# A hybrid encoder block on one core: attention on the normed latent, row sums through DRAM, squares on GpSimd

## The chip, the cores and the metric

The kernel runs on one core of a Trainium2 chip. A core has five engines with instruction queues of their own: TensorE (PE in the profile, its weight loads as PEld), VectorE (DVE), ScalarE (ACT), GpSimd (POOL) and SyncE (SP), which in this kernel issues all DMAs. The metric is the time of one execution in device microseconds, as a median over runs. All tensors are f32.

## The reference

One encoder layer, on 2048 tokens of 1024 features:

```python
h = x
xn = rms_norm(h, ln_mix_g)
proj = xn @ w_in            # q, k, v, o: 512 columns each; 16 gates; c_q 256; c_kv 128; k_rope 64
y_a = mlstm_group(...)      # 4 heads of 128, both directions, chunks of 128 tokens
# multi-head latent attention, 4 heads
q = (rms_norm(c_q, q_norm_g) @ w_uq).reshape(b, s, 4, 128 + 64)
kv = (rms_norm(c_kv, kv_norm_g) @ w_ukv).reshape(b, s, 4, 128 + 128)
k_nope, v = kv[..., :128], kv[..., 128:]
sc = q_nope . k_nope + rope(q_rope) . rope(k_rope)     # k_rope is one for all heads
y_b = softmax(sc * (128 + 64) ** -0.5) @ v
h = h + concat(y_a, y_b) @ w_out
h = h + conv_gated_mlp(rms_norm(h, ln_ffn_g), ...)     # 1024 -> 2 x 2816 -> 1024
h = h + sigmoid(rms_norm(h, ple_norm_g) @ w_ple_gate) * rms_norm(p @ w_ple_proj, ple_post_g)
out = rms_norm(h, final_g)
```

Two products of the attention group are linear on both sides. The score q_nope . k_nope of a head is c_q W_uq (W_uk)^T c_kv^T, and what a head adds to h is (softmax @ c_kv) W_uv W_out, where c_kv is the normed latent of 128 columns that all heads share.

## The kernel before

Most products are made with operands split into a high part (ScalarE's cast to fp32r) and a low part (VectorE's subtraction): `split` (L111 to L118) makes the parts, `mm3` (L128) three matmuls from them. The tiles live at named places (`at("w13", ...)`), most with one buffer, so a place that is taken again waits for its last reader. A list scheduler orders each engine's instructions from the program; only in the q and k projection is TensorE's order that of the program. All DMAs stand in SP's one queue, and one that waits holds those behind it.

The stages, in order of time:

- `in_proj`, first part. For each of 16 token tiles of 128, `turn_in` splits the tile of x and `ssq_x` (L224 to L234) makes its mean square: ScalarE squares into `x_sq` (128 features x 8 x 128 tokens, place w13), VectorE sums over the 8 blocks (L229) into `x_ss` (place t7), TensorE sums over the partitions (L231) and GpSimd raises to -1/2 (L234, `rcol`). `rest` (L242 to L269) projects the 464 columns of gates, c_q, c_kv and k_rope, norms c_q and c_kv into `nn` (GpSimd L257, and L136, L138 in `rsq`; VectorE L259, L260) and applies the rope (VectorE L262 to L268). `turn_rest` transposes `nn` and stores it to `rest_d`.
- Then v and o, each 16 token tiles.
- Then q and k: 8 column blocks (j) of 4 token blocks (c), each 24 matmuls, with the convolution over tokens behind them (`conv`). Between the matmuls a side generator is pumped, 1.14 steps at a time: `kv_up`, then `gates`, then `q_up`. `kv_up` loads the latent, projects it with w_ukv to keys (features x tokens, `ko`, stored to `k_d`) and values (tokens x features, `vo2`, stored to `vv_d`) for all heads, 96 matmuls into `gb`. `q_up` does the queries (`q_d`). At j = 7 the keys of head 0 are loaded (`load_kv`) and split (`split_kv`), and a tail behind the loop splits its values.
- `attend` (L823 on): 64 tiles (head h, 128 queries qt). The work of a tile is written out in a string, L912: scores of the next tile (s0 to s3, L849 to L853, with the row maximum L854), exponentials of this and the next (E, e, L872), transposes of the exponentials (t0 to t3, L889, with a split behind each), and V, half of the product with the values for a pair of tiles (`ppv`). At each "." the mLSTM group is pumped. After the fourth exponential the sum over keys is inverted (`ri`, L877, L878) and spread over a row of 128 (`rb`, L881); at R of an odd tile `turn_sums` (L923 to L929) transposes the two `rb` of the pair and copies them to SBUF (`rbs`), and L905 multiplies the finished `ppv` by it and stores it to `y_d`. The keys and values of the next head are loaded and split eight times a head during the head before. The `mk` masks of the mLSTM are made on GpSimd (L765), its `kk` by VectorE (L705) for the products of L712.
- `out_proj`, with the w_out rows loaded and split by `load_wo`, the first four of them during the last head; then the gated MLP (`up`, `down`) and `ple`.

Of the kernel before, what the change touches and what calls it, by code (L numbers as in the profile page):

```python
# [18 lines left out]
P = 128  # L19
# [40 lines left out]
class Block:  # L60
# [4 lines left out]
    def __init__(self, ctx, tc, d):  # L65
# [15 lines left out]
        self.kv = {}  # L81
# [5 lines left out]
        self.k_d = dt([NH, P, S], F32, name="k_d")  # L87
        self.vv_d = dt([NH, P, S], F32, name="vv_d")
# [90 lines left out]
    def in_proj(self):  # L179
# [44 lines left out]
        def ssq_x(st, x_t):  # L224

            sq = self.at("w13", [P, KT, P], name="x_sq")
            nc.scalar.activation(sq, x_t, AF.Square)
            ss = self.at("t7", [P, P], name="x_ss")
            nc.vector.tensor_reduce(ss, sq.rearrange("p k t -> p t k"), axis=AX.X, op=ALU.add)  # L229
            ps = self.pml.tile([P, 4], F32, name="ssp", tag="ml")  # L230
            nc.tensor.matmul(ps, ss, ones, start=True, stop=True)  # L231
# [10 lines left out]
        def rest(st):  # L242
# [17 lines left out]
            nc.vector.scalar_tensor_tensor(nn[:, 256:384], rs[:, 256:384], r[:, 1:2], gn[:, 256:384], op0=ALU.mult, op1=ALU.mult)  # L260
            x1, x2 = rs[:, 384:416], rs[:, 416:448]
# [75 lines left out]
        side, due = chain(self.kv_up(), self.gates(), self.q_up()), 0.0  # L337
# [16 lines left out]
        def pump(due):  # L354
            due += 1.14
            while due >= 1:
                next(side, None)
                due -= 1
            return due
# [12 lines left out]
        with self.tc.manual_schedule(engines={mybir.EngineType.PE}):  # L372
            nxt = load_qk(0)
            for j in range(8):
                ws = nxt
                if j < 7:
                    nxt = load_qk(j + 1)
                else:
                    kr = self.load_kr()
                    kv = [self.load_kv(0, i, w) for i, w in enumerate(("w8", "w13", "w9", "w12"))]  # L380
# [4 lines left out]
                for c in order:  # L385
# [18 lines left out]
                    if j == 7 and c == 1:  # L404
                        for _ in self.split_kv(0, kv, range(2)):
                            pass
# [5 lines left out]
        def tail():  # L412
            for c in (1, 0):
                conv(7, u, c)
                yield
            yield from pause(4)
            yield from self.split_kv(0, kv, range(2, 4))
# [42 lines left out]
    def kv_up(self):  # L460
        nc, d = self.nc, self.d
        wh, wl = self.at("w3", [P, 1024], F32R, "wkh"), self.at("w4", [P, 1024], F32R, "wkl")
        for i in range(2):
            raw = self.at(("t4", "t5")[i], [P, 512], name="wkr")
            fs = slice(i * 512, (i + 1) * 512)
            nc.sync.dma_start(raw, d["w_ukv"][0, :, fs])
            self.split(raw, wh[:, fs], wl[:, fs])
        vw = [w.rearrange("p (h c) -> p h c", h=NH)[:, :, P:2 * P] for w in (wh, wl)]
        orot = _rot("t", (6, 7, 4, 5))

        def load(c):
            raw = self.at(("w8", "w13")[c % 2], [P, 512], name="craw")
            nc.sync.dma_start(raw, self.rest_d[:, 2, c * 512:(c + 1) * 512])
            cc = self.at(("w5", "w7")[c % 2], [P, 2, 512], F32R, "ckv")
            self.split(raw, cc[:, 0], cc[:, 1])
            return cc

        nxt = load(0)
        yield
        for c in range(4):  # L480
            sl = slice(c * 512, (c + 1) * 512)
            ch, cl = nxt[:, 0], nxt[:, 1]
            if c < 3:
                nxt = load(c + 1)
            for h in range(NH):
                ps = self.gbank()
                ws = slice(h * 256, h * 256 + P)
                self.mm3(ps, wh[:, ws], wl[:, ws], ch, cl, True, True)
                o = self.at(next(orot), [P, 512], name="ko")
                nc.scalar.copy(o, ps)  # L490
                nc.sync.dma_start(self.k_d[h, :, sl], o)
                if h % 2:
                    yield
            for t in range(4):
                ps = self.gbank()
                ts = slice(t * P, (t + 1) * P)
                self.mm3(ps.rearrange("p (h c) -> p h c", h=NH), ch[:, ts], cl[:, ts], vw[0], vw[1], True, True)
                o = self.at(next(orot), [P, 512], name="vo2")
                nc.scalar.copy(o, ps)
                tk = slice((c * 4 + t) * P, (c * 4 + t + 1) * P)  # L500
                nc.sync.dma_start(self.vv_d[:, :, tk].rearrange("h p e -> p h e"), o.rearrange("p (h e) -> p h e", h=NH))
                if t % 2:
                    yield
# [319 lines left out]
    def attend(self, side):  # L823
        nc = self.nc
        mm = nc.tensor.matmul
        prot, ptrot = _rot("w", (0, 1, 2)), _rot("x", range(8, 14))
        kv, qv, rbp = self.kv, {}, {}
# [14 lines left out]
        def score_bank(s, kb):  # L842
# [5 lines left out]
            kh, kl = kv[h][0], kv[h][1]  # L848
# [20 lines left out]
        def expo(s, kb):  # L869
# [5 lines left out]
            if kb == 3:  # L875
# [3 lines left out]
                if s.qt % 2 == 0:  # L879
                    rbp[s.h, s.qt // 2] = self.at(f"s{(s.qt // 2) % 2}", [P, 2, P], name="rb")  # L880
                nc.vector.tensor_copy(rbp[s.h, s.qt // 2][:, s.qt % 2, :], ri.broadcast_to([P, P]))  # L881
# [10 lines left out]
        def pv(w, half):  # L892
# [3 lines left out]
            vh, vl = kv[h][2], kv[h][3]  # L896
# [26 lines left out]
        def turn_sums(h, pr):  # L923
            pb = self.tbank([P, 2, P])
            for i in range(2):
                nc.tensor.transpose(pb[:, i, :], rbp[h, pr][:, i, :], self.ident)
            rb = self.at("s2", [P, 2, P], name="rbs")
            nc.scalar.copy(rb, pb)
# [11 lines left out]
        loads = iter(())  # L940
        pts, pend = [], None
        for i, (h, qt) in enumerate(seq):
            if qt == 1 and h + 1 < NH:
                loads = self.split_kv(h + 1, None, range(4))
            next(loads, None)
# [12 lines left out]
            for op in order:  # L958
# [6 lines left out]
                elif op == "R" and qt % 2:  # L965
                    rb = turn_sums(h, qt // 2)
# [586 lines left out]
```

## Time and profile before

| | us |
|---|---|
| median of 3 runs | 3047.44 (3045.35 to 3048.96) |
| the profiled execution | 3049.62 |
| its span, first to last instruction | 3047.8 |
| TensorE busy | 2987.7 (98%) |
| VectorE busy | 1928.1 (63%) |
| ScalarE busy | 1381.3 (45%) |
| GpSimd busy | 138.6 (5%) |

By stage of that execution, in us:

| stretch | what runs | length | TensorE | VectorE | ScalarE | GpSimd |
|---|---|---|---|---|---|---|
| 0 to 97 | `rest` projection | 97 | 84.3 | 80.7 | 63.1 | 31.9 |
| 97 to 270 | v and o | 173 | 169.2 | 40.3 | 30.9 | 3.8 |
| 270 to 530 | q and k, with the side work | 260 | 257.8 | 135.2 | 122.1 | 0.0 |
| 530 to 1280 | attention and mLSTM | 750 | 727.4 | 576.1 | 455.7 | 45.7 |
| 1280 to 1460 | w_out | 180 | 180.0 | 79.9 | 53.7 | 13.4 |
| 1460 to 3047.8 | MLP, `ple` | 1587.8 | 1569.1 | 1015.9 | 656.0 | 43.8 |

In the profile's rows a group reads: line, engine, operation, result <- operands, shapes and count, and then times. A row of a wait reads: engine, what it was about to do, "<-" the work that released it, the sum in us, how often, and the longest. An engine's q (SPq) is its instruction queue, where DMAs are issued. A matmul's duration is that of a pipelined instruction; the distance of two starts is what it costs a full TensorE. An f32 product that is not split stands in the trace as two matmul records. The granted clock of TensorE was 0.997 of full speed on the mean.

### The profile page before, as it was taken

To read this page: it belongs to the slowest core of one execution; us is meant where nothing else is said; L and a number is where in the kernel's file an instruction comes from. 1 tells how busy PE (TensorE), PEld (TensorE's weight loads), DVE (VectorE), ACT (ScalarE), POOL (GpSimd) and SP (SyncE) were. 2 spreads that over 40 slices of the span, in tenths; PEclk is the share of its full clock that TensorE was granted. 3 is DMA by queue.
4 is the path that set the end of the run, shared out by engine and by line. 5 is a ranking of instruction groups with operands and counts; after the bars stand their busy time and mean duration, and the time that the engine had idled before them with its cause. 6 is when DMAs were issued, how large, how long until landed. Compare 5 with 4: busy or idle time off the path is not lost. (4 is left out here: it accounts for less than half of the span.)

```text
span 3047.8 us, 40996 instructions
## 1 busy us (share of the span) xinstructions
PE 2987.7 (98%) x15208; PEld 2520.1 (83%) x15208; DVE 1928.1 (63%) x3527; ACT 1381.3 (45%) x2642; POOL 138.6 (5%) x262
## 2 busy tenths in 40 slices
PE   8999999899999999999999999999999999999999
PEld 7788888788898898888778887788887888888887
DVE  8321555778777787734798888877777343334555
ACT  7212544556666565522544445544444332223444
POOL 3100000000000000000000000000000000000111
PEclk9999999999999999999999999999999999999999
DMA  6522445444333243458763335433336565444221
GB/s 175 114 69 98 149 132 168 143 128 150 101 108 114 95 133 92 137 195 280 255 224 137 135 136 190 145 125 125 124 125 227 166 221 200 145 155 151 78 78 62
DMA packets 332264, 441.03 MB, mean 145 GB/s; under 512 B 25296, under 2 KB 224928, under 8 KB 332064
## 3 DMA queue, kind: packets, MB, share of 16 engines
q1 hardware_dynamic: 332064, 438.42, 44.7%
q8 instruction: 119, 1.95, 0.3%
q14 instruction: 81, 0.66, 0.1%
HBM read 295.84 MB, written 142.50 MB: 144 GB/s over the span
## 5 line engine op out<-in xcount | busy, mean ns | idle before, releaser
L128 PE MATMUL facc<-fw,hid 128*128 128x512 f32 x2112 | 480.7, 390 | 3.0 <-ACT fw L115 1.4
L128 PEld LDWEIGHTS facc<-fw,hid 128*128 128x128 f32 x2112 | 396.2, 188 | 86.6 <-ACT fw L115 1.9
L128 PE MATMUL fxy<-oph,fw 128*128 128x512 f32 x1408 | 450.4, 393 | 7.1 <-DVE ug L1313 4.6
L128 PEld LDWEIGHTS fxy<-oph,fw 128*128 128x128 f32 x1408 | 264.4, 188 | 76.0 <-DVE ug L1313 10.6
L118 DVE TENSOR_TENSOR fw<-fwr,fw 128x1024 fp32r<-128x1024 f32 x176 | 215.2, 1223 | 165.4 <-ACT fw L115 165.4
L115 ACT CAST fw<-fwr 128x1024 fp32r<-128x1024 f32 x176 | 184.7, 1050 | 255.9 <-PE facc L128 131.5
L128 PE MATMUL fxy<-opl,fw 128*128 128x512 f32 x704 | 275.1, 391 | 0.0
L128 PE MATMUL bk<-wsp,xh 128*128 128x512 f32 (+1 forms) x768 | 235.3, 387 | 1.0 <-DVE wsp L124 1.0
L128 PE MATMUL fzs<-oph,fw 128*128 128x512 f32 x704 | 234.5, 390 | 0.0
L115 ACT CAST pt<-tb 128x512 fp32r<-128x512 f32 x256 | 146.1, 588 | 186.4 <-PE tb L889 185.6
L128 PE MATMUL ppv<-pt,kv 128*128 128x256 f32 x1536 | 203.7, 287 | 0.0
L854 DVE TENSOR_REDUCE mx<-bk 128x1 f32<-128x512 f32 x256 | 174.9, 684 | 34.1 <-PE bk L853 33.3
L118 DVE TENSOR_TENSOR pt<-tb,pt 128x512 fp32r<-128x512 f32 x256 | 173.6, 685 | 35.5 <-ACT pt L115 33.9
L128 PEld LDWEIGHTS ppv<-pt,kv 128*128 128x128 f32 x1536 | 188.9, 191 | 0.0
L128 PE MATMUL pgp<-pw,x3s 128*128 128x512 f32 (+1 forms) x792 | 178.7, 385 | 0.0
L872 ACT ACTIVATE pe<-bk,nm 128x512 f32<-128x512 f32 x256 | 173.9, 697 | 10.2 <-DVE nm L866 9.4
L128 PE MATMUL bk<-wo,yhl 128*128 128x512 f32 x744 | 174.3, 392 | 0.0
L128 PE MATMUL bk<-xh,wqk 128*128 128x512 f32 x512 | 169.1, 394 | 0.0
L128 PEld LDWEIGHTS pgp<-pw,x3s 128*128 128x128 f32 x792 | 144.5, 188 | 28.2
L128 PEld LDWEIGHTS bk<-wsp,xh 128*128 128x128 f32 x768 | 144.6, 189 | 27.6 <-DVE wsp L124 2.7
L128 PEld LDWEIGHTS bk<-wo,yhl 128*128 128x128 f32 x744 | 138.4, 188 | 28.1
L128 PE MATMUL bk<-wsp,xl 128*128 128x512 f32 (+1 forms) x384 | 149.7, 390 | 7.9 <-ACT wsp L123 7.3
(321 smaller groups left out, 5465.1 us busy)
## 6 DMA issues: line engine op xcount, KB each, us to landing
fwr<-in_w_down SPq DMA_DIRECT2D x88, 512.0 KB, 3.9
fwr<-in_w_up SPq DMA_DIRECT2D x66, 512.0 KB, 3.9
s_d<-fwr SPq DMA_DIRECT2D x44, 512.0 KB, 3.2
fws<-s_d SPq DMA_DIRECT2D x44, 512.0 KB, 3.6
hraw<-hid_d SPq DMA_DIRECT2D x33, 512.0 KB, 4.8
rw<-row_d SPq DMA_DIRECT2D x32, 512.0 KB, 5.2
hid_d<-fgv SPq DMA_DIRECT2D x22, 512.0 KB, 3.6
hid_d<-fgv SPq DMA_DIRECT2D x22, 511.5 KB, 5.1
```

Of the source, the lines that this page charges most:

```text
L115: nc.scalar.copy(hi, src)
L118: (sub or nc.vector).tensor_tensor(lo, src, _f(hi), op=ALU.subtract)
L128: mm = lambda *a, **k: self.nc.tensor.matmul(*a, **k, skip_group_check=more)
L854: nc.vector.tensor_reduce(s.mx[:, kb:kb + 1], ps, axis=AX.X, op=ALU.max)
L872: nc.scalar.activation(s.pe[:, kb % 2], s.banks[kb], AF.Exp, bias=s.nm, scale=ASCALE, accum_out=s.rs[:, kb:kb + 1])
```

## The change

Three things are changed.

First, `absorb` replaces `kv_up`. It multiplies w_uq's 128 unrotated columns of each head by the head's key weights (8 unsplit f32 products into `gb`, two copies back into `wqr`, which `q_up` then splits as before), and each head's value weights by its 128 rows of w_out (a split of 128x1024, a split of 128x128, two `mm3` of 128x512, copies `woo`, stored to `wo_d`). Attention then takes the normed latent as keys (from `rest_d`) and as values (from `vv_d`, now written tile by tile in `rest` out of `nn`) for all heads: it is split once, in four quarters, and the loads and splits per head are gone. The host hands over w_uq and w_ukv with heads turned. The high and low exponentials `pt` take the places x8, x9, x4 to x7 in place of x8 to x13, and `load_wo` takes x0 to x7 in order and its last four blocks from `wo_d`. The pump's step is 1.17 in place of 1.14.

Second, `turn_sums` is gone: each tile's `ri` (128 x 1) is stored to `ri_d`, and at R of an odd tile a DMA loads the pair's 256 sums back, broadcast over the partitions, into `rbs` (places s0 to s2).

Third, in `ssq_x` three GpSimd additions of 512, 256 and 128 elements a partition stand in place of VectorE's reduction.

In the diff, the removed body of `kv_up` and context are cut; the body stands in the functions above.

```diff
@@ -78,14 +78,14 @@
         dt = self.dram.tile
-        self.kv = {}
         self.qk_d = dt([NT, P, 8, P], F32, name="qk_d")
...
         self.q_d = dt([NH, 8, P, 2, 256], F32, name="q_d")
-        self.k_d = dt([NH, P, S], F32, name="k_d")
-        self.vv_d = dt([NH, P, S], F32, name="vv_d")
+        self.vv_d = dt([P, NT, P], F32, name="vv_d")
+        self.wo_d = dt([NH, P, D], F32, name="wo_d")
+        self.ri_d = dt([NH, NT, P], F32, name="ri_d")
         self.cb_d = dt([NT, P, NH, 129], F32, name="cb_d")
@@ -225,8 +225,11 @@
             nc.scalar.activation(sq, x_t, AF.Square)
+            add = lambda o, a, b: nc.gpsimd.tensor_tensor(o, a, b, op=ALU.add)
+            add(sq[:, 0:4], sq[:, 0:4], sq[:, 4:8])
+            add(sq[:, 0:2], sq[:, 0:2], sq[:, 2:4])
             ss = self.at("t7", [P, P], name="x_ss")
-            nc.vector.tensor_reduce(ss, sq.rearrange("p k t -> p t k"), axis=AX.X, op=ALU.add)
+            add(ss, sq[:, 0], sq[:, 1])
             ps = self.pml.tile([P, 4], F32, name="ssp", tag="ml")
@@ -258,6 +261,7 @@
             nc.vector.scalar_tensor_tensor(nn[:, 256:384], rs[:, 256:384], r[:, 1:2], gn[:, 256:384], op0=ALU.mult, op1=ALU.mult)
+            nc.sync.dma_start(self.vv_d[:, st], nn[:, 256:384])
             x1, x2 = rs[:, 384:416], rs[:, 416:448]
@@ -334,7 +338,7 @@
         H = S // 2
-        side, due = chain(self.kv_up(), self.gates(), self.q_up()), 0.0
+        side, due = chain(self.absorb(), self.gates(), self.q_up()), 0.0
         urot, wrot = _rot("u", (0, 1, 2)), _rot("w", (6, 9, 10, 11))
@@ -352,7 +356,7 @@
         def pump(due):
-            due += 1.14
+            due += 1.17
             while due >= 1:
@@ -377,7 +381,7 @@
                     kr = self.load_kr()
-                    kv = [self.load_kv(0, i, w) for i, w in enumerate(("w8", "w13", "w9", "w12"))]
+                    kv = [self.load_kv(i, w) for i, w in enumerate(("w8", "w13", "w9", "w12"))]
                 u = [self.at(next(urot), [P, H + 2], name="u") for _ in range(2)]
@@ -401,8 +405,8 @@
                         self.split_kr(kr)
-                    if j == 7 and c == 1:
-                        for _ in self.split_kv(0, kv, range(2)):
+                    if j == 7 and c == 2:
+                        for _ in self.split_kv(kv, range(2)):
                             pass
@@ -414,7 +418,7 @@
             yield from pause(4)
-            yield from self.split_kv(0, kv, range(2, 4))
+            yield from self.split_kv(kv, range(2, 4))
@@ -438,79 +442,80 @@
-    def load_kv(self, h, i, place):
+    def load_kv(self, i, place):
...
         raw = self.at(place, [P, 1024], name="kvr")
-        self.nc.sync.dma_start(raw, (self.k_d, self.vv_d)[i // 2][h, :, (i % 2) * 1024:(i % 2) * 1024 + 1024])
+        hs = slice((i % 2) * 1024, (i % 2) * 1024 + 1024)
+        self.nc.sync.dma_start(raw, self.vv_d.rearrange("p k c -> p (k c)")[:, hs] if i // 2 else self.rest_d[:, 2, hs])
         return raw
...
-    def split_kv(self, h, raws, quarters):
-        t = self.kv.setdefault(h, [None] * 4)
+    def split_kv(self, raws, quarters):
         for i in quarters:
-            a = i // 2 * 2
+            a = i // 2
             if i % 2 == 0:
-                t[a:a + 2] = [self.at(f"x{4 - (h % 2) * 4 + a + b}", [P, S], F32R, f"kv{a + b}") for b in range(2)]
-            raw = raws[i] if raws else self.load_kv(h, i, "w13")
+                t = [self.at(f"x{12 - 2 * a + b}", [P, S], F32R, f"kv{a}{b}") for b in range(2)]
+                if a:
+                    self.vh, self.vl = t
+                else:
+                    self.kh, self.kl = t
+            hi, lo = (self.vh, self.vl) if a else (self.kh, self.kl)
             for e in range(2):
                 sl = slice((i % 2) * 1024 + e * 512, (i % 2) * 1024 + e * 512 + 512)
-                self.split(raw[:, e * 512:e * 512 + 512], t[a][:, sl], t[a + 1][:, sl])
+                self.split(raws[i][:, e * 512:e * 512 + 512], hi[:, sl], lo[:, sl])
                 yield
...
-    def kv_up(self):
+    def absorb(self):
         nc, d = self.nc, self.d
...
+        mm = nc.tensor.matmul
+        uq = self.at("w3", [P, NH, 256], name="uqt")
+        nc.sync.dma_start(uq, d["w_uq_turned"])
+        uk, uv = [self.at(("t4", "t5")[i], [P, NH, P], name="ukvt") for i in range(2)]
+        for i, t in enumerate((uk, uv)):
+            nc.sync.dma_start(t, d["w_ukv_turned"][:, i])
+        self.wqr = []
+        for kt in range(2):
+            r = self.at(("w13", "w4")[kt], [P, 768], name="wqr")
+            nc.sync.dma_start(r, d["w_uq"][0, kt * P:(kt + 1) * P, :])
+            self.wqr.append(r)
+
+        def load(h):
+            r = self.at("w8", [P, D], name="wor")
+            nc.sync.dma_start(r, d["w_out"][0, 512 + h * P:512 + (h + 1) * P, :])
+            return r
+
+        raw = load(0)
+        yield from pause(3)
+        for kt in range(2):
+            ps = self.gbank([P, NH, P])
             for h in range(NH):
+                mm(ps[:, h], uq[:, h, kt * P:(kt + 1) * P], uk[:, h], start=True, stop=True)
+            nc.scalar.copy(self.wqr[kt].rearrange("p (h c) -> p h c", h=NH)[:, :, 0:P], ps)
+            yield
+        for h in range(NH):
+            wh, wl = [self.at(t, [P, D], F32R, "woa") for t in ("w5", "w7")]
+            self.split(raw, wh, wl)
+            if h + 1 < NH:
+                raw = load(h + 1)
+            us = self.at(f"s{h % 2}", [P, 2, P], F32R, "uvs")
+            self.split(uv[:, h], us[:, 0], us[:, 1])
+            yield from pause(2)
+            for hf in range(2):
+                fs = slice(hf * 512, hf * 512 + 512)
                 ps = self.gbank()
-                ws = slice(h * 256, h * 256 + P)
-                self.mm3(ps, wh[:, ws], wl[:, ws], ch, cl, True, True)
-                o = self.at(next(orot), [P, 512], name="ko")
+                self.mm3(ps, us[:, 0], us[:, 1], wh[:, fs], wl[:, fs], True, True)
+                o = self.at(f"t{6 + hf}", [P, 512], name="woo")
                 nc.scalar.copy(o, ps)
-                nc.sync.dma_start(self.k_d[h, :, sl], o)
-                if h % 2:
-                    yield
-            for t in range(4):
-                ps = self.gbank()
-                ts = slice(t * P, (t + 1) * P)
-                self.mm3(ps.rearrange("p (h c) -> p h c", h=NH), ch[:, ts], cl[:, ts], vw[0], vw[1], True, True)
-                o = self.at(next(orot), [P, 512], name="vo2")
-                nc.scalar.copy(o, ps)
-                tk = slice((c * 4 + t) * P, (c * 4 + t + 1) * P)
-                nc.sync.dma_start(self.vv_d[:, :, tk].rearrange("h p e -> p h e"), o.rearrange("p (h e) -> p h e", h=NH))
-                if t % 2:
-                    yield
+                nc.sync.dma_start(self.wo_d[h, :, fs], o)
+            yield
...
         for kt in range(2):
-            r = self.at(("w8", "w13")[kt], [P, 768], name="wqr")
-            nc.sync.dma_start(r, d["w_uq"][0, kt * P:(kt + 1) * P, :])
-            w = [self.at(("w3", "w4", "w5", "w7")[2 * kt + i], [P, 768], F32R, "wq") for i in range(2)]
-            self.split(r, w[0], w[1])
+            w = [self.at(("w3", "w5", "w7", "w2")[2 * kt + i], [P, 768], F32R, "wq") for i in range(2)]
+            self.split(self.wqr[kt], w[0], w[1])
             wq.append(w)
@@ -823,8 +828,8 @@
         mm = nc.tensor.matmul
-        prot, ptrot = _rot("w", (0, 1, 2)), _rot("x", range(8, 14))
-        kv, qv, rbp = self.kv, {}, {}
+        prot, ptrot = _rot("w", (0, 1, 2)), _rot("x", (8, 9, 4, 5, 6, 7))
+        kh, kl, qv = self.kh, self.kl, {}
         self.wo = []
@@ -845,7 +850,6 @@
             ps = self.bank()
-            kh, kl = kv[h][0], kv[h][1]
             mm(ps, q[:, 1, o:o + P], kh[:, ks], start=True, stop=False)
@@ -876,9 +880,7 @@
                 nc.vector.reciprocal(ri, ri)
-                if s.qt % 2 == 0:
-                    rbp[s.h, s.qt // 2] = self.at(f"s{(s.qt // 2) % 2}", [P, 2, P], name="rb")
-                nc.vector.tensor_copy(rbp[s.h, s.qt // 2][:, s.qt % 2, :], ri.broadcast_to([P, P]))
+                nc.sync.dma_start(self.ri_d[s.h, s.qt].unsqueeze(1), ri)
@@ -893,7 +895,7 @@
                 w.ps = self.ppv.tile([P, 256], F32, name="ppv", tag="pv")
-            vh, vl = kv[h][2], kv[h][3]
+            vh, vl = self.vh, self.vl
             for kb in (2 * half, 2 * half + 1):
@@ -920,12 +922,10 @@
-        def turn_sums(h, pr):
-            pb = self.tbank([P, 2, P])
-            for i in range(2):
-                nc.tensor.transpose(pb[:, i, :], rbp[h, pr][:, i, :], self.ident)
-            rb = self.at("s2", [P, 2, P], name="rbs")
-            nc.scalar.copy(rb, pb)
+        def sums(h, pr):
+
+            rb = self.at(f"s{pr % 3}", [P, 2, P], name="rbs")
+            self.row_bcast(rb.rearrange("p a t -> p (a t)"), self.ri_d[h, 2 * pr:2 * pr + 2].rearrange("a t -> (a t)"), 2 * P)
             return rb
@@ -937,12 +937,8 @@
             expo(cur, int(o[1]))
-        loads = iter(())
         pts, pend = [], None
         for i, (h, qt) in enumerate(seq):
-            if qt == 1 and h + 1 < NH:
-                loads = self.split_kv(h + 1, None, range(4))
-            next(loads, None)
             if h == NH - 1 and qt in (4, 6, 8, 10):
@@ -963,7 +959,7 @@
                 elif op == "R" and qt % 2:
-                    rb = turn_sums(h, qt // 2)
+                    rb = sums(h, qt // 2)
                 elif op == "X" and nxt:
@@ -1010,8 +1006,8 @@
         raw = self.at("w13" if k < 4 else ("w13", "w12")[k % 2], [P, D], name="wor")
-        nc.sync.dma_start(raw, self.d["w_out"][0, k * P:(k + 1) * P, :])
-        w = self.at(f"x{(k + 4) % 8}", [P, 2, D], F32R, f"wo{k}")
+        nc.sync.dma_start(raw, self.d["w_out"][0, k * P:(k + 1) * P, :] if k < 4 else self.wo_d[k - 4])
+        w = self.at(f"x{k}", [P, 2, D], F32R, f"wo{k}")
         self.split(raw, w[:, 0], w[:, 1])
@@ -1540,6 +1536,10 @@
     turned = lambda a: _np.ascontiguousarray(a.T.reshape(-1, P, S).transpose(1, 0, 2))
+    heads = lambda a, n, o=0: a[0].reshape(-1, NH, n)[:, :, o:o + P].transpose(2, 1, 0)
+    src["w_uq_turned"] = _np.ascontiguousarray(heads(src["w_uq"], 192))
+    ukv = src.pop("w_ukv")
+    src["w_ukv_turned"] = _np.ascontiguousarray(_np.stack([heads(ukv, 256), heads(ukv, 256, P)], axis=1))
     src["g_turned"] = _np.ascontiguousarray(src.pop("ln_mix_g")[0].reshape(KT, P).T)
```

More of the change, by code (lines that the diff above doesn't have):

```diff
@@ L454, in split_kv @@
             for e in range(2):
                 sl = slice((i % 2) * 1024 + e * 512, (i % 2) * 1024 + e * 512 + 512)
-                self.split(raw[:, e * 512:e * 512 + 512], t[a][:, sl], t[a + 1][:, sl])
+                self.split(raws[i][:, e * 512:e * 512 + 512], hi[:, sl], lo[:, sl])
                 yield
-    def kv_up(self):
+    def absorb(self):
         nc, d = self.nc, self.d
-        wh, wl = self.at("w3", [P, 1024], F32R, "wkh"), self.at("w4", [P, 1024], F32R, "wkl")
-        for i in range(2):
[L464 to L478, printed above, removed]
-        yield
[L480 to L484, printed above, removed]
-            for h in range(NH):
@@ L488, in kv_up @@
-                self.mm3(ps, wh[:, ws], wl[:, ws], ch, cl, True, True)
-                o = self.at(next(orot), [P, 512], name="ko")
+                self.mm3(ps, us[:, 0], us[:, 1], wh[:, fs], wl[:, fs], True, True)
+                o = self.at(f"t{6 + hf}", [P, 512], name="woo")
                 nc.scalar.copy(o, ps)
-                nc.sync.dma_start(self.k_d[h, :, sl], o)
-                if h % 2:
-                    yield
-            for t in range(4):
-                ps = self.gbank()
-                ts = slice(t * P, (t + 1) * P)
-                self.mm3(ps.rearrange("p (h c) -> p h c", h=NH), ch[:, ts], cl[:, ts], vw[0], vw[1], True, True)
-                o = self.at(next(orot), [P, 512], name="vo2")
-                nc.scalar.copy(o, ps)
-                tk = slice((c * 4 + t) * P, (c * 4 + t + 1) * P)
-                nc.sync.dma_start(self.vv_d[:, :, tk].rearrange("h p e -> p h e"), o.rearrange("p (h e) -> p h e", h=NH))
-                if t % 2:
-                    yield
+                nc.sync.dma_start(self.wo_d[h, :, fs], o)
@@ L921, in pump @@
                 due[0] -= 1
-        def turn_sums(h, pr):
-            pb = self.tbank([P, 2, P])
-            for i in range(2):
-                nc.tensor.transpose(pb[:, i, :], rbp[h, pr][:, i, :], self.ident)
-            rb = self.at("s2", [P, 2, P], name="rbs")
-            nc.scalar.copy(rb, pb)
+        def sums(h, pr):
+            rb = self.at(f"s{pr % 3}", [P, 2, P], name="rbs")
+            self.row_bcast(rb.rearrange("p a t -> p (a t)"), self.ri_d[h, 2 * pr:2 * pr + 2].rearrange("a t -> (a t)"), 2 * P)
             return rb
```

## The prediction, made before the changed kernel ran

> **What bounds the kernel now.** I read the page's first part, then the table by stage, then what TensorE waited for, and only then the groups that the diff touches.
>
> ```profile
> span 3047.8 us, 40996 instructions
> PE 2987.7 (98%) x15208; PEld 2520.1 (83%) x15208; DVE 1928.1 (63%) x3527; ACT 1381.3 (45%) x2642; POOL 138.6 (5%) x262
> ...
> 10.00:97.00 87.00, 81.64 (x413) 70.28 (x411) 76.74 (x214) 57.60 (x127) 31.25 (x55) 1.00 0.60 158
> ...
> 270.00:530.00 260.00, 257.84 (x1303) 217.42 (x1302) 135.20 (x364) 122.06 (x229) 0.00 (x0) 1.00 0.49 149
> 530.00:570.00 40.00, 30.02 (x150) 24.74 (x150) 29.00 (x66) 24.24 (x52) 0.00 (x0) 0.87 0.48 153
> 570.00:1280.00 710.00, 697.33 (x4759) 627.88 (x4759) 547.10 (x1444) 431.45 (x1173) 45.72 (x64) 1.00 0.37 116
> ```
>
> In the stage rows the busy times stand in the order PE, PEld, DVE, ACT, POOL, then the granted clock. TensorE idles 60 us of 3047.8. So a matmul taken away is worth its pitch wherever it sat in a full queue (270 to 530, 570 to 1280), and work moved between the other engines is worth nothing there. Two places are not full: the stage of the `rest` projection (10 to 97), where VectorE is nearly as busy as TensorE, and the passage into attention (530 to 570). The waits say the same:
>
> ```profile
> PE mb L712 <- DVE kk L705: 6.4, 1, 6.4
> PE ssp L231 <- DVE x_ss L229: 4.7, 10, 1.3
> ```
>
> **Part 1: key and value up-projection folded into the weights.** Gone are the 96 matmuls into `gb` that read `ckv`:
>
> ```profile
> L128 PE MATMUL gb<-ckv,wkh x32: 389/390/390, 291.5 to 326.4; 128*128 128x512 f32 x32
> L128 PE MATMUL gb<-wkh,ckv x32: 388/390/390, 296.7 to 330.5; 128*128 128x512 f32 x32
> ...
> L128 PE MATMUL gb<-ckv,wkl x16: 389/390/390, 291.2 to 325.9; 128*128 128x512 f32 x16
> ...
> L128 PE MATMUL gb<-wkl,ckv x16: 389/390/390, 296.9 to 330.2; 128*128 128x512 f32 x16
> ```
>
> The 0.39 us is a pipelined duration; the price is the start-to-start pitch. In time order around the first of them:
>
> ```profile
> 291.01 0.39 PE L128 MATMUL bk<-xh,wqk 128*128 128x512 f32 x1
> 291.24 0.39 PE L128 MATMUL gb<-ckv,wkl 128*128 128x512 f32 x1
> 291.46 0.61 PE L128 MATMUL gb<-ckv,wkh 128*128 128x512 f32 x2
> ```
>
> 291.01, 291.24, 291.46: 0.225 to 0.23 each, so 96 x 0.227 = 21.8 us. Added are 2 x 3 matmuls of the same 128x512 form per head for `woa`, 24 x 0.227 = 5.4 us, and 8 unsplit f32 products of 128x128 for the query weights. The nearest form is the unsplit f32 product of L774, of which the trace shows two records each:
>
> ```profile
> 703.30 1.06 PE L774 MATMUL mb<-qk 128*128 128x128 f32 x8
> 704.12 0.48 PE L849 MATMUL bk<-kv,q_t 128*128 128x512 f32 x1
> ```
>
> Eight records take 0.82 us, 0.103 each; 16 make 1.6 us, 3.3 if there are four records to a product. Sum of part 1 on TensorE: -21.8 + 5.4 + 1.6 = **-14.8 us**. It lies wholly in the stage 270 to 530, which is 99% full, so I count all of it.
>
> Everything else in part 1 sits off the path: the 16 `ko` and 16 `vo` copies and 24 of the 32 splits of k and v go from ScalarE and VectorE, which have 138 and 125 us to spare in 270 to 530 and 279 and 163 in attention; in come four splits of w_out rows, four small ones and ten copies. From SP's queue 32 stores and 12 reloads of k and v go; eight stores of the new w_out rows come, and 16 stores of `nn` (64 KB) join the `rest` stage, where the DMA share is 0.60. I cost these at nothing; their cover is those idle shares. The pump's step of 1.17 moves side work a few slots earlier in a full queue: nothing.
>
> **Part 2: row sums by way of DRAM.** Gone are `turn_sums`' 64 transposes, 32 copies on ScalarE (L928, below) and 64 broadcast copies on VectorE (L881).
>
> ```profile
> L926 PE MATMUL tb<-ident,rb x64: 269/273/329, 562.6 to 1276.3; 128*128 128x128 f32 x64
> its engine sat idle before it (us, times) until:
>   DVE rb L881: 3.6, 4
>   DVE pt L118: 0.9, 2
> ...
> 628.78 0.38 PE L926 MATMUL tb<-ident,rb 128*128 128x128 f32 x2
> ...
> 629.00 0.28 PE L712 MATMUL mb<-v,kk 128*128 128x129 f32 x1
> ```
>
> A pair takes 629.00 - 628.78 = 0.22 us; 32 pairs make **-7.0 us**. The 4.5 us of idle before them is a wait on VectorE. What is late next is the transposes of `pe` right behind, which need the same VectorE queue, so I count **-3** of it (ends -4.5 and 0).
>
> In its place: a store of 128 sums per tile and a broadcast load per pair, 96 DMAs on SP. The nearest rows:
>
> ```profile
> y_d<-rbs SPq DMA_DIRECT2D x64, 64.0 KB, 1.7
> ...
> gcol<-in_g_turned SPq DMA_DIRECT2D x1, 4.0 KB, 1.6
> ...
> r_d<-rcol SPq DMA_DIRECT2D x1, 8.0 KB, 11.4
> ...
> L905 DVE TENSOR_TENSOR rbs<-rbs,ppv x32: 404/421/423, 579.3 to 1283.1; 128x256 f32<-128x256 f32 x32
> ...
> L928 ACT COPY rbs<-tb x32: 353/372/392, 563.8 to 1276.6; 128x256 f32<-128x256 f32 x32
> ```
>
> `rcol` is 2048 single elements in 11.4 us; 128 of them lie nearer `gcol`'s 1.6. Store and load in a row are then about 1.6 + 1.7 = 3.3 us, at worst 11.4 + 1.7 = 13.1. The first consumer, L905, runs at 579.3, 15.5 us after the copy at 563.8 that the load replaces. So it is hidden unless SP is held up. SP does stand still for long:
>
> ```profile
> SPq L832 <- PE bk L853: 97.4, 24, 13.6
> SPq L743 <- PE mb L789: 67.7, 12, 15.1
> ```
>
> Now the load waits on SP for its own store to land, 1.6 us or more, 32 times, and the loads of `q_t` and of the mLSTM side that stand behind it come that much later; most of them wait longer than that for TensorE anyway. I take **+1** (ends 0 and +10).
>
> **Part 3: squares summed on GpSimd.** Every tile loses one VectorE reduction, and GpSimd gets adds of 512, 256 and 128 elements:
>
> ```profile
> L229 DVE TENSOR_REDUCE x_ss<-x_sq x16: 1935/1990/2019, 11.6 to 86.3; 128x128 f32<-128x1024 f32 x16
> ...
> L765 POOL TENSOR_SCALAR_AFFINE_SELECT mk<-rw x32: 630/636/1314, 689.1 to 1231.3; 128x512 f32<-128x512 f32 x32
> ...
> masks.py:199 POOL TENSOR_SCALAR_AFFINE_SELECT ident<-ident 128x128 f32<-128x128 f32 x1 | 0.3, 292 | 0.1
> ...
> 59.24 1.51 POOL L257 TENSOR_SCALAR ssq<-ssq 128x1 f32<-128x1 f32 x1 [1.60 <-ACT nn L256]
> ...
> 65.94 0.22 POOL L257 TENSOR_SCALAR ssq<-ssq 128x1 f32<-128x1 f32 x1 [0.97 <-ACT nn L256]
> ```
>
> No large two-input add on GpSimd is in the trace. From the one-input pair, 0.636 at 512 and 0.292 at 128, the slope is 0.9 ns an element with 0.18 us fixed: 3 x 0.18 + 896 x 0.9 ns = 1.3 us as the lower end. With two operands read one after the other the slope doubles: 2.15 us, which I take. The stage row gives GpSimd's other work as 31.25 / 16 = 1.95 us a tile, so it has then 4.1 of the 5.4 us that a tile lasts (87 us by 16).
>
> But the two engines get in each other's way: the single-element L257 lasted 1.51 us at 59.24, against 0.22 at 65.94, while VectorE ran its subtractions and rope products of two SBUF operands back to back. Without L229 VectorE works 76.74 / 16 - 1.99 = 2.8 us a tile. If GpSimd had to stand aside for all of that, its tile would be 4.1 + 2.8 = 6.9 us; if for half, 5.5. So the stage stays near its period or goes a little over. VectorE, 88% busy there, loses 2 us a tile, and the 4.7 us that TensorE waits for L229 may go. Bounds: -4.7 below, 16 x (6.9 - 5.4) = +24 above; I take **+3**, the middle of GpSimd's waiting (0.1 to 0.2 us a tile over the period).
>
> The Trainium skill bears on this in "SBUF — State Buffer", section "SBUF: two separate sides": VectorE with two SBUF inputs and GpSimd reading SBUF take a shared port pair by exclusive lock, for a whole instruction. The 1.51 us row agrees. Its "GPSIMD Engine Reference", section 3.1, puts a two-input add at about 2.6 cycles an element; an estimate by that is 896 x 2.6 / 1.2 GHz plus the fixed part, some 2.5 us a tile, and the sum would be up to 6 us higher.
>
> **The passage into attention.** In time order:
>
> ```profile
> 536.49 0.69 DVE L118 TENSOR_TENSOR kv<-kvr,kv 128x512 fp32r<-128x512 f32 x1 [1.79 <-ACT kv L115]
> ...
> 542.33 0.68 DVE L705 SCALAR_TENSOR_TENSOR kk<-kk,cols 128x512 f32<-128x512 f32 x1
> ...
> 546.45 0.63 PE L850 MATMUL bk<-kr,q_t 128*128 128x512 f32 x1
> 546.87 0.63 PE L851 MATMUL bk<-kv,q_t 128*128 128x512 f32 x1
> ...
> 551.23 0.39 PE L850 MATMUL bk<-kr,q_t 128*128 128x512 f32 x1
> ```
>
> VectorE sits with splits of k and v and reaches `kk` at 542.33; TensorE idles 6.4 us and then runs at half pace (starts 0.43 apart instead of 0.23) to about 551, some 4 us more. After the change the splits of head 1 are gone here, but splits of w_out can come in, and the splits of the latent's value half stay. I take **-3** (ends -10 and 0).
>
> **Sum**, against the profiled execution's 3049.6 us (span 3047.8 and 1.8 around it): -14.8 - 7.0 - 3 + 1 + 3 - 3 = -23.8, giving 3025.8. That execution is 2.2 us above the median shown, so the median goes from 3047.4 to **3024 us**. No change means within 0.2%, 6 us.
>
> **Rivals.**
> - *GpSimd becomes the bound of the `rest` stage.* For: the 1.51 us row, and one buffer each for `x_sq` and `x_ss`, so the next square waits for the adds. Against: VectorE has two fifths of its work less there (1.99 of 4.8 us a tile), and part of that reads a single operand. With a tile of 6.4 us it is +16 instead of +3: 3037. It takes back everything from 7.1 us a tile on (26.8 us without this term, by 16, is 1.7 over 5.4), just past the worst of part 3. Chance 0.17.
> - *Row sums come late* (slower). SP held 13 to 15 us, as in the L743 row, ahead of the store or load, plus the 3.3 us use up the 15.5 us; then L905 stands at the head of VectorE's queue, with the maxima and `pt` splits behind it, and TensorE waits for those. It decides from 24.8 / 32 = 0.78 us a pair; at 1 us it gives 3055. Against: SP's waits end when TensorE moves on, and only a pair whose stall falls just there is hit. Chance 0.08.
> - *The passage closes wholly*: -10 instead of -3, and VectorE's relief takes the last waits in attention: 3014. Chance 0.12.
> - *The removed products were no path*, other waits taking their place: within 6 us of 3047. The 98% row speaks against it. Chance 0.03.
>
> **How the numbers follow.** My forecast has 0.60, its own range 3016 to 3031. Faster: 0.60 + 0.12 + 0.14 of the first rival = 0.86; same: 0.03 + 0.01 = 0.04; slower: 0.08 + 0.02 = 0.10. The range 3010 to 3042 leaves out the late sums and the worst of GpSimd.
>
> **What would show it.** In the profile after: the stage 270 to 530 about 15 us shorter at the same TensorE share; attention's tiles 0.11 us shorter with no wait at L905 for a DMA; the `rest` stage 87 us plus or minus 5, GpSimd busy 4 to 5 us a tile; TensorE's wait at L712 below 6.4. Wrong would be a `rest` stage above 110 us, or VectorE waiting for `rbs` once a pair.

## The result, and the profile after

The changed kernel takes 3169.51 us (median of 4 runs, 3166.85 to 3175.43) against 3047.16 us: a ratio of 1.0404, with a 95% interval of 1.0386 to 1.0422. I had forecast 3024 us, a gain of 0.8%; it is a loss of 4%. The profiled execution's span is 3166.5 us. From its page:

```profile
PE 3011.0 (95%) x15088; PEld 2529.2 (80%) x15088; DVE 1890.0 (60%) x3425; ACT 1350.3 (43%) x2566; POOL 175.7 (6%) x310
```

and the table by stage, with the stages' own bounds (columns as before: length, then PE, PEld, DVE, ACT, POOL, the granted clock, the DMA share, GB/s):

```profile
0.00:308.90 308.90, 277.15 (x1250) 229.60 (x1250) 109.82 (x304) 95.89 (x204) 74.07 (x118) 0.98 0.37 103
308.90:543.80 234.90, 227.71 (x1172) 191.60 (x1172) 139.46 (x371) 112.30 (x208) 0.00 (x0) 1.00 0.47 145
543.80:1378.50 834.70, 746.56 (x4803) 662.37 (x4801) 539.80 (x1402) 428.99 (x1158) 45.29 (x64) 0.96 0.56 99
1378.50:1582.70 204.20, 198.43 (x951) 164.43 (x950) 92.25 (x116) 63.74 (x102) 13.46 (x30) 0.98 0.74 239
1582.70:3166.50 1583.80, 1561.15 (x6918) 1281.15 (x6916) 1008.68 (x1235) 649.37 (x896) 42.84 (x98) 1.00 0.45 150
```

The same five stages of before:

```profile
0.00:288.30 288.30, 271.77 (x1249) 226.72 (x1249) 123.72 (x320) 97.20 (x204) 35.69 (x70) 1.00 0.38 107
288.30:531.40 243.10, 240.94 (x1228) 203.65 (x1229) 133.89 (x365) 120.23 (x226) 0.00 (x0) 1.00 0.51 155
531.40:1283.10 751.70, 729.04 (x4927) 654.57 (x4926) 575.08 (x1505) 454.51 (x1223) 45.72 (x64) 0.99 0.38 119
1283.10:1469.30 186.20, 186.20 (x882) 154.09 (x882) 84.70 (x105) 59.33 (x97) 14.11 (x30) 1.00 0.74 243
1469.30:3047.80 1578.50, 1559.75 (x6927) 1281.08 (x6925) 1010.68 (x1237) 650.06 (x896) 43.05 (x98) 1.00 0.45 151
```

So the projections of rest, v and o lost 20.6 us, q and k won 8.2, attention lost 83.0, the stage of w_out 18.0 and the rest 5.3. The 18.0 are in part work that only changed its place: TensorE has 951 records in the stage of w_out, where it had 882. In attention the DMA engines are busier (0.56 against 0.38) and move less (99 GB/s against 119). That pair of numbers is the trace's main clue. TensorE idles for longer and its granted clock is 0.96 there in place of 0.99, so its busy time grows although it has fewer products to do. The waits that matter, of SP's queue and then of TensorE (sum in us, times, longest):

```profile
SPq L142 <- DMA ri_d<-ri: 209.9, 32, 10.6
```

```profile
PE bk L853 <- ACT pe L876: 32.0, 9, 5.2
...
PE ssp L234 <- POOL x_ss L228: 11.8, 7, 3.0
```

and the DMA issues (count, KB each, median us to landing), first after, then before:

```profile
q_t<-q_d SPq DMA_DIRECT2D x32, 256.0 KB, 5.8
...
y_d<-hy SPq DMA_DIRECT2D x16, 256.0 KB, 7.8
...
ri_d<-ri SPq DMA_DIRECT2D x64, 0.5 KB, 8.1
```

```profile
q_t<-q_d SPq DMA_DIRECT2D x32, 256.0 KB, 2.7
...
y_d<-hy SPq DMA_DIRECT2D x16, 256.0 KB, 2.4
```

A store of half a kilobyte takes 8.1 us, and most other transfers of attention take about twice as long as before or more, also those that stand nowhere near the wait on SP; a few hardly change (`rw`, the rows for the masks, 6.0 us in place of 5.2). ScalarE, which makes the exponentials, waits in attention for the queries to arrive, first after, then before:

```profile
ACT q_t L115 <- DMA q_t<-q_d: 78.0, 25, 6.9
```

```profile
ACT q_t L115 <- DMA q_t<-q_d: 10.5, 10, 1.8
```

### The profile page after: what moved, and what is told of

Its sections match the earlier page's. It is cut to its first block, busy times and chain, and to the rows that moved or that the text cites. A ratio compares the mean times of both kernels' runs of the same rounds, so it can differ in the third digit from the quotient of the medians.

```text
span 3166.5 us, 40748 instructions
## 1 busy us (share of the span) xinstructions
PE 3011.0 (95%) x15088; PEld 2529.2 (80%) x15088; DVE 1890.0 (60%) x3425; ACT 1350.3 (43%) x2566; POOL 175.7 (6%) x310
## 5 line engine op out<-in xcount | busy, mean ns | idle before, releaser
L891 PE MATMUL tb<-ident,pe 128*128 128x128 f32 x1024 | 155.5, 279 | 4.9 <-DVE pt L118 4.9
```

What stands on the lines that cost most here:

```text
L891: nc.tensor.transpose(t[:, j, :], s.p[kb][:, j * P:(j + 1) * P], self.ident)
```

## The experiments

My first theory was that part 2 holds most of the loss, part 3 some 20 us, and that part 1 keeps its gain. The rival was that part 1, with other buffers and later splits, is itself slower. Of the first four kernels three do one part each, and the fourth takes a piece of part 2 by itself. All ran on one chip, on which before takes 3055.11 us.

**Part 1 alone**: the changed kernel with the lines of parts 2 and 3 put back.

```diff
-                nc.sync.dma_start(self.ri_d[s.h, s.qt].unsqueeze(1), ri)
+                nc.vector.tensor_copy(rbp[s.h, s.qt // 2][:, s.qt % 2, :], ri.broadcast_to([P, P]))
...
-                    rb = sums(h, qt // 2)
+                    rb = turn_sums(h, qt // 2)
...
-            add(ss, sq[:, 0], sq[:, 1])
+            nc.vector.tensor_reduce(ss, sq.rearrange("p k t -> p t k"), axis=AX.X, op=ALU.add)
```

> Part 1 alone: the weights absorb the up-projections, the sums are turned on TensorE and the squares are reduced on VectorE as before. My theory is that part 1 keeps its gain and the loss of the whole change lies in parts 2 and 3: about 3033 us, 14 below before (3030 to 3040). The rival is that part 1 itself holds the loss, by other places for the buffers and a split that comes later: then 3080 or more.

Measured: 3050.09 us, ratio 0.9989 (0.9980 to 0.9998). The rival falls: part 1 loses nothing. But it wins only some 5 us of the 14 expected; where the rest went is taken up below.

**Part 2 alone**, on the kernel before (the first two edits above, the other way round).

> Part 2 alone, on the kernel before. In the changed kernel's trace the stage from the first score to the first product with w_out is 83 us longer and SP stands 210 us behind the stores of the sums. My theory puts this on part 2: 3130 to 3150. If the rows came cheaply, as I had predicted, it would be 3040; if the loss needs part 1 too, below 3080.

Measured: 3229.75 us, ratio 1.0569 (1.0552 to 1.0587): 175 us lost, more than expected and more than the whole change loses.

**Part 3 alone**, on the kernel before.

> Part 3 alone, on the kernel before. In the changed kernel's trace q and k begin 20.6 us later (308.9 against 288.3). My theory puts all of it on the GpSimd additions: 3065 to 3070. If part of it belongs to the 16 stores of nn that part 1 puts into that stage, 3050 to 3060.

Measured: 3074.19 us, ratio 1.0061 (1.0046 to 1.0076), some 4 us more than expected, and q and k begin at 308.8: the 20 us of the first stage are all part 3's. The last stage, which part 3 doesn't touch, takes 1584.8 us here, so the 5.3 us that it lost in the changed kernel aren't traced to the change.

**Dead stores**: part 1 alone, and one line more.

```diff
+                nc.sync.dma_start(self.ri_d[s.h, s.qt].unsqueeze(1), ri)
                 if s.qt % 2 == 0:
                     rbp[s.h, s.qt // 2] = self.at(f"s{(s.qt // 2) % 2}", [P, 2, P], name="rb")
```

> As the kernel with part 1 alone, and besides each tile's 128 sums are stored to DRAM as in the change, but nothing reads them: no load stands behind them on SP. If the harm is that the load waits on SP for the store to land (8.1 us) and holds the queue, this kernel runs within 5 us of part 1 alone. If the stores of single elements themselves slow the other transfers, it is 40 us or more above it.

Measured: 3213.50 us, ratio 1.0516 (1.0501 to 1.0532), 163 us above part 1 alone. Nothing waits for these stores, and yet nearly the whole loss is there, so the wait on SP isn't what makes it. In this kernel's order of time on SP, and its windows around one store:

```profile
633.63 0.38 SPq L880 DMA_DIRECT2D ri_d<-ri  x1
634.11 0.38 SPq L728 DMA_DIRECT2D kTb<-qk_d  x1
635.86 0.32 SPq L732 DMA_DIRECT2D kn_d<-kk  x1
640.25 0.52 SPq L695 DMA_DIRECT2D v<-v_d  x1
```

```profile
632.00:635.00 3.00, 3.00 (x18) 2.52 (x17) 0.00 (x0) 0.05 (x1) 0.00 (x0) 1.00 0.68 218
635.00:637.00 2.00, 0.40 (x2) 0.00 (x0) 1.62 (x4) 1.32 (x3) 0.00 (x0) 1.00 0.86 202
637.00:643.00 6.00, 3.57 (x23) 2.96 (x23) 4.40 (x13) 0.59 (x1) 0.00 (x0) 1.00 0.74 30
643.00:645.00 2.00, 0.74 (x4) 0.74 (x5) 0.27 (x1) 0.86 (x2) 0.00 (x0) 0.64 0.72 227
645.00:647.00 2.00, 2.00 (x11) 2.00 (x10) 1.11 (x2) 1.59 (x4) 0.00 (x0) 0.50 0.10 38
```

With 256 KB transfers issued before and after it, the DMA engines stay 74% busy from 637 to 643 and move 30 GB/s in place of over 200. The store of 512 bytes brings the other transfers nearly to a halt. TensorE runs dry twice in these windows. The 1.8 us before 637 end with `kk`, which is late because ScalarE stood 3.4 us for the load of `q_t`. The 3.5 us before 644 end with ScalarE's copy of `rbs`, which stood 4.9 us until the store of the last `rbs` to `y_d`, issued at 633.22, had landed and left its place free. The granted clock is 0.64 and 0.50 after that. Over all of attention that second way costs (TensorE, then ScalarE):

```profile
PE tb L891 <- ACT rbs L930: 19.0, 7, 3.9
```

```profile
ACT rbs L930 <- DMA y_d<-rbs: 27.9, 6, 6.5
```

A store that meets no other transfer shows the same from another side. One is issued at 593.24; five transfers of 256 KB follow from 598.13 to 600.75:

```profile
594.00:599.00 5.00, 5.00 (x32) 4.30 (x31) 3.29 (x8) 0.59 (x1) 0.00 (x0) 1.00 0.04 2
599.00:603.00 4.00, 4.00 (x33) 3.71 (x32) 3.74 (x9) 2.65 (x5) 0.00 (x0) 1.00 0.20 28
603.00:607.00 4.00, 4.00 (x27) 3.61 (x26) 1.26 (x5) 2.38 (x8) 0.00 (x0) 1.00 0.88 315
```

They hardly move before 603, nearly 10 us after the store, and then at 315 GB/s. The DMA share is low here (0.04 and 0.20), so a high share is not a sure sign of the stall; a low rate while transfers stand issued is. TensorE had work at hand and lost nothing this time.

What in the store does that: its 128 elements, their size of 4 bytes, or that they lie side by side in DRAM? Three more kernels on part 1 with dead stores differ in that alone, and the whole change ran beside them, on a second chip (before: 3053.02 us). Part 1 alone did not run there; its ratio to before, 0.9989, is what they are set beside.

> The whole change once more, beside the other kernels on one chip. The dead stores alone cost 163 us over part 1, the three parts singly -5, +175 and +19. If the parts simply add, 3240 here; if the whole change holds back other transfers while SP waits for the store, and so loses less, it stays near 3170.

Measured: 3204.20 us, ratio 1.0495 (1.0464 to 1.0525). Between the two figures expected: the parts don't quite add. This is the median of only two runs, and why the same kernel loses more here than in the first measurement (1.0404) isn't shown.

**512 and 64 bytes from sum to sum**, here the second:

```diff
-        self.ri_d = dt([NH, NT, P], F32, name="ri_d")
+        self.ri_d = dt([NH, NT, P, 16], F32, name="ri_d")
...
+                nc.sync.dma_start(self.ri_d[s.h, s.qt, :, 0:1], ri)
```

> Part 1 and dead stores of the same 128 four-byte sums a tile, but each sum goes to an address of its own 512 bytes from the next. If the stall comes from 128 small writes to one and the same 512 bytes of DRAM, the stores land in about 2 us and the time is within 10 us of part 1 alone. If it comes from the number or the smallness of the elements, it is again 150 us or more above part 1 alone.

> The same with 64 bytes from sum to sum, so that eight sums share 512 bytes and a store covers 8 KB, as the store of rcol in the kernel before does with 2048 sums. If only writes to the same 512 bytes stand in line, eight instead of 128 of them cost little: within 25 us of part 1 alone. If smallness counts, 150 us or more above.

Measured: 3047.54 us (ratio 0.9980, 0.9968 to 0.9991) and 3046.19 us (0.9983, 0.9971 to 0.9995): as part 1 alone. The 64 stores of 128 four-byte elements now cost nothing. From the DMA issues of the kernel with 64 bytes:

```profile
q_t<-q_d SPq DMA_DIRECT2D x32, 256.0 KB, 2.9
...
ri_d<-ri SPq DMA_DIRECT2D x64, 0.5 KB, 1.4
```

1.4 us to land, against 9.1 with the sums side by side. So neither count nor size does the harm by itself: many small writes close together in DRAM do. 64 bytes apart is far enough; I tried nothing between 4 and 64. Why neighbouring addresses are so slow, and where in the path the writes stand in line, isn't shown.

**One row of 512 bytes** from one partition, to the same address and of the same size (its values are others, which nothing reads):

```diff
+                nc.sync.dma_start(self.ri_d[s.h, s.qt].unsqueeze(0), rbp[s.h, s.qt // 2][0:1, s.qt % 2, :])
```

> Part 1 and dead stores of 512 bytes as one row from one partition (the sums spread by VectorE, as they are for the turning on TensorE): as many stores, as many bytes, one element each. If the count of the stores or the address did the harm, it stays; if the small elements do it, this runs within 5 us of part 1 alone.

Measured: 3045.73 us, ratio 0.9980 (0.9969 to 0.9991). The place isn't at fault either, once the bytes come in one piece.

The last four ask what is left of parts 1 and 3, and whether part 2 can be had without its fault (before: 3056.32 us).

**Two buffers for the squares**, on part 3 alone:

```diff
-            sq = self.at("w13", [P, KT, P], name="x_sq")
+            sq = self.at(("w13", "u0")[st % 2], [P, KT, P], name="x_sq")
...
-            ss = self.at("t7", [P, P], name="x_ss")
+            ss = self.at(("t7", "u1")[st % 2], [P, P], name="x_ss")
```

> Part 3 alone on the kernel before, with two buffers each for the squares and their sum, so that ScalarE may write the next square while GpSimd adds. Part 3 alone cost 19 us. If the single buffers make the chain of square, additions and sum that long, most of it comes back: below 3060 where before is 3055. If GpSimd and VectorE stand in each other's way, as the 1.48 us of a 0.49 us norming step in the changed kernel's trace suggests, it stays: 3068 or more.

Measured: 3070.01 us, ratio 1.0042 (1.0027 to 1.0057). q and k begin at 305.2 in place of 308.8: by one execution of each, the single buffers are 3.6 of the 20 us, and the rest stays. The two intervals overlap, so the 3.6 is uncertain. The changed kernel's order of time shows GpSimd's and VectorE's side of it (two additions merged in the first row):

```profile
40.04 2.14 POOL L228 TENSOR_TENSOR x_sq<-x_sq 128x512 f32<-128x512 f32 x2
42.26 0.98 POOL L228 TENSOR_TENSOR x_ss<-x_sq 128x128 f32<-128x128 f32 x1
```

```profile
40.11 1.48 DVE L262 SCALAR_TENSOR_TENSOR nn<-rs,rsr,gn 128x256 f32<-128x256 f32 x1 [1.20 <-POOL rsr L138]
41.52 0.81 DVE L263 SCALAR_TENSOR_TENSOR nn<-rs,rsr,gn 128x128 f32<-128x128 f32 x1
```

and from the groups of the kernel before and of part 3 alone, the norming step (ns min, median, max):

```profile
L259 DVE SCALAR_TENSOR_TENSOR nn<-rs,rsr,gn x16: 468/485/488, 26.4 to 119.1; 128x256 f32<-128x256 f32 x16
```

```profile
L262 DVE SCALAR_TENSOR_TENSOR nn<-rs,rsr,gn x13: 483/675/1520, 30.0 to 113.4; 128x256 f32<-128x256 f32 x13
```

A step that never took more than 0.49 us takes up to 1.52 beside the additions, and the last addition, 0.49 us by its median, takes 0.98 beside VectorE. The three additions take 1.30 + 0.80 + 0.63 = 2.7 us a tile on the mean of the changed kernel's groups, against VectorE's 1.99, and GpSimd's other work comes after them in the same chain.

**The additions on VectorE**, on part 1 alone:

```diff
-            add = lambda o, a, b: nc.gpsimd.tensor_tensor(o, a, b, op=ALU.add)
+            add = lambda o, a, b: nc.vector.tensor_tensor(o, a, b, op=ALU.add)
```

> Part 1, with the three additions on VectorE in place of its reduction. From the row of the split (512 elements, two operands, 0.69 us) the three take some 0.69 + 0.4 + 0.25 = 1.3 us against 1.99. If the additions are harmful only on GpSimd, 0 to 5 us below part 1 alone (3045 to 3050 where before is 3055); if their chain as such is harmful, above it.

Measured: 3053.99 us, ratio 0.9994 (0.9984 to 1.0003); q and k begin at 291.7, against 290.6 with part 1 alone. Three additions in place of one reduction can't be told from the reduction by the time; the gain that I thought possible didn't come. On GpSimd they cost 20 us. How much of that is their length and how much the mutual hold-up isn't separated.

**The pump's step at 1.14**, on part 1 alone (one number).

> Part 1 with the pump's step at 1.14 as before. Part 1 alone has 5 us more idle time on TensorE among q and k than the kernel before, most of it before the transposes of the rotated queries (4.8 against 1.2 us). If the denser pumping is the cause, 3 to 5 us below part 1 alone; if the order of the DMAs on SP is, the same time.

Measured: 3051.50 us, ratio 0.9983 (0.9974 to 0.9993). TensorE's wait before the transposes of the rotated queries falls from 4.8 to 2.1 us and the stage from 236.8 to 235.4, but the time can't be told from part 1 alone: unclear.

**Row sums by another way**, on part 1 alone: single elements into a row of SBUF, then one piece of 1 KB to DRAM for a pair, and the broadcast load at V in place of R.

```diff
-                nc.vector.tensor_copy(rbp[s.h, s.qt // 2][:, s.qt % 2, :], ri.broadcast_to([P, P]))
+                nc.sync.dma_start(rbp[s.h, s.qt // 2][0:1, s.qt % 2, :], ri)
...
+        def put_row(h, pr):
+            nc.sync.dma_start(self.ri_d[h, 2 * pr:2 * pr + 2].unsqueeze(0), rbp[h, pr][0:1])
```

> Part 1, and row sums by way of DRAM in another form: the 128 sums of a tile go as single elements into one row of SBUF, and a pair's 256 sums go from there to DRAM as one piece of 1 KB and come back broadcast. If only small writes to one place of DRAM stall the transfers, this saves TensorE's 7 us of turning: 3040 to 3048 where before is 3055. If small writes into SBUF stall them too, 3150 or more; if the longer chain of three DMAs makes the rows late, 3060 to 3100.

Measured: 3038.69 us, ratio 0.9944 (0.9929 to 0.9959): the fastest of all, 18 us below before and a little under what was expected. Its table has attention at

```profile
528.10:1253.50 725.40, 709.82 (x4802) 639.50 (x4801) 542.47 (x1403) 427.12 (x1158) 45.79 (x64) 1.00 0.38 115
```

against 739.6 us with part 1 alone. The small writes into SBUF cost nothing here, and three DMAs in a row still come in time.

## Why the prediction was wrong

- **Row sums by way of DRAM, +1 (0 to +10): the step that failed.** Alone it costs 175 us, its stores alone 163. I priced the store by the row of `gcol` ("128 of them lie nearer `gcol`'s 1.6"), which is a load in rows of 32 bytes a partition, and took `rcol`, the only store of single elements in the trace, for no more than the worst landing. And I treated it as a latency that either fits into 15.5 us or doesn't. It is a stall of the core's other transfers, and their lateness reaches TensorE. The trace of before shows that too, in windows that the prediction doesn't look at; its store of `rcol` is issued at 92.49:

```profile
92.00:97.00 5.00, 5.00 (x28) 4.45 (x26) 1.84 (x11) 1.49 (x6) 1.61 (x4) 1.00 0.88 28
97.00:102.00 5.00, 5.00 (x27) 4.42 (x24) 0.19 (x2) 0.00 (x0) 0.00 (x0) 1.00 1.16 21
```

  A full DMA share (by this measure even over 1) and 21 to 28 GB/s. It reaches TensorE as well: the store to `rest_d` issued right behind `rcol`, at 92.98, holds its buffer, ScalarE waits 11.0 us for it, and TensorE for ScalarE:

```profile
PE rtp L274 <- ACT rt L276: 2.8, 1, 2.8
```

  There it happens once, in the changed kernel 64 times; 64 x 2.8 = 179 us would have been an estimate from the trace of before. That it comes so near to the 163 to 175 measured is partly luck, since not every store costs TensorE anything. Nor does the number of elements set the time: `rcol` has 16 times as many, in 16 such pieces of 512 bytes, and took 11.4 us against 8 to 9.
- **Late sums, the slower rival**: its sign came true, its mechanism not. L907 never waits for the row sums; the loads of `q_t` and `kk` are late (in attention ScalarE's wait for `q_t` grows from 10.5 to 78.0 us, and VectorE waits 40.1 us for `kk` in the changed kernel against 1.2 in the whole of the kernel before), and the scores with them. So the sign of being wrong that I had named here, VectorE waiting for `rbs`, never came, though the time was wrong. SP's standing still adds little: dead stores without it cost 163 us over part 1, part 2 with it 175 over before.
- **turn_sums, -7.0 and -3 of the idle before it: right.** With the row through SBUF attention and w_out take 725.4 + 195.9 = 921.3 us, with part 1 alone 739.6 + 196.1 = 935.7: 14.4 less, some more than the 10 I had counted. TensorE's busy time is 12.4 of it, in part by the clock, which is 0.91 in place of 0.83 in the first 40 us. The base of the -3 was misread: the 4.5 us of idle are mostly waits of the weight loads, and TensorE's own wait there is 1.6, so that the -3 fits is partly luck.
- **Squares on GpSimd, +3 (-4.7 to +24): the rival came true, the term was too small.** Measured 20 us, near the upper end: 1.3 us a tile over the 5.4, so 6.7, between the rival's 6.4 and the worst of 6.9. The additions take 2.7 us a tile, where I took 2.15 by doubling a slope. The estimate by the Trainium skill's "GPSIMD Engine Reference" (section 3.1), 2.5, was the nearer one. And I let GpSimd wait for VectorE, but not VectorE for GpSimd; the 1.48 us row (0.49 undisturbed) shows that it happens. The exclusive lock that the Trainium skill states in "SBUF — State Buffer", section "SBUF: two separate sides", works both ways, and that row agrees. GpSimd is not full: with part 3 alone it is busy 59.6 of the 87 us from 10 to 97, VectorE 55.9. I read the loss as a chain of additions, norms and TensorE's sum that grew longer than a tile; that is argued, not shown by a kernel of its own.
- **Part 1, -14.8 on TensorE: half of it.** With part 1 alone q and k take 236.8 us in place of 243.1, 6.3 less. TensorE's busy time there falls by 11.8 (240.94 to 229.17), and its idle time grows from 2.2 to 7.6, by waits I had set at nothing: 3.6 more before the transposes of the rotated queries, 0.9 each for `woa` and `uqt`; after the longest the granted clock is 0.83 for 10 us. (The 243.1 are from the first measurement; part 3 alone, on the same chip as part 1 alone, has 243.3.)
- **The passage into attention, -3: not seen.** The wait for `kk` falls from 6.4 to 2.1 us, as expected, but the first 40 us of attention run at a clock of 0.83 in place of 0.87, and attention with w_out takes 935.7 us against 935.8 with part 3 alone on the same chip.

## What to carry to other kernels

Before a small store is added, look in the trace for a store of the same shape, and at what the DMA engines moved while it ran: a few GB/s while larger transfers stand issued, often at a high DMA share, is a stall that the other transfers pay, and not only a latency of the store that slack can hide. Many four-byte writes side by side in DRAM did that here; as many bytes in one piece, the same writes 64 bytes apart, or the sums gathered in SBUF first, cost nothing. Work handed to GpSimd beside a busy VectorE should be costed as a chain and in both directions, not by the idle share of GpSimd.

## What the hardware showed that I had not expected

- 128 writes of 4 bytes into 512 bytes of DRAM take 8 to 9 us to land and hold up the core's other transfers (30 GB/s at a DMA share of 0.74 with transfers under way); the same 128 writes 64 bytes apart land in 1.4 us, and the kernel loses no time by them.
- 64 of them made a kernel in which TensorE was 98% busy 163 us slower: with transfers late, TensorE ran dry in many short gaps, and after one of them the granted clock was as low as 0.50.
